# Top-10 indices of 8192 rows: result rows gathered by one-hot matmuls into one store a batch, and the last tile handled by itself

## The chip, the core and the metric

The kernel runs on one core of one Trainium2 chip. The metric is the device time of one execution in microseconds, median of several. A profiled execution also gives the span: first instruction to last. It is about 2 us below the timed figure (721.4 against 723.2 for the same run). A second figure beside each span is the mean clock granted to TensorE (PE).

## The reference

```python
x = np.random.randn(8192, 8192).astype(np.float32); k = 10
indices = np.argpartition(x, -k, axis=1)[:, -k:]
values = np.take_along_axis(x, indices, axis=1)
sorted_idx = np.argsort(-values, axis=1)
return np.take_along_axis(indices, sorted_idx, axis=1)     # int64, (8192, 10)
```

All 268 MB of x have to be read once; the result is 0.66 MB.

## The kernel before

64 tiles of 128 rows pass through a pipeline. A tile lies in SBUF, the on-chip memory of 128 partitions, with each row cut into 16 pieces of 512 columns: partition `(a q)` holds piece q of 16 rows, one after the other, and eight such sets `a` make the 128 rows. `load` brings 4 MB in four DMAs of 1 MB; `weigh` takes exponentials on ScalarE (ACT) and sums them over the 16 pieces of a row with matmuls; `choose` finds the 12 best of 512 columns on VectorE (DVE); `gather` (GpSimd, POOL) fetches the values at these columns; `spread` and `extract` (DVE, PE) line up a row's 192 candidates; `rank`, three tiles later, finds the ten best; once in eight tiles `decode` makes indices of the positions and `store` sends them.

```python
P = 128; N = 8192; R = 16; A = 8; S = 16; W = 512; KMAX = 10; G = 12; TB = 8; LAG = 3
# pools are laid out in SBUF in this order; input tiles come last
consts = tile_pool(name="consts", bufs=1)
epool  = tile_pool(name="e", bufs=3)
small  = tile_pool(name="small", bufs=2)
bpool  = tile_pool(name="batch", bufs=2)
xpool  = tile_pool(name="x", bufs=4)
# ...
def load(t):
    xts[t] = xpool.tile([P, N], fp32, tag="xt", name="xt")
    src = x[t*P:(t+1)*P, :].rearrange("(s a) (q j) -> (a q) s j", a=A, q=R)
    dst = xts[t].rearrange("p (s j) -> p s j", j=W)
    n = S // 4
    for s in range(0, S, n):
        nc.sync.dma_start(out=dst[:, s:s+n, :], in_=src[:, s:s+n, :])
# ...
def decode(b):
    # ... slot, low, hot, pick
    o = opacks[b % 2]                                   # [P, TB, KMAX, 2] u32
    nc.vector.scalar_tensor_tensor(out=o[:, :, :, 0], in0=low, scalar=float(W), in1=pick,
                                   op0=ALU.mult, op1=ALU.add)
    ready[b] = o

def store(b):
    o = ready.pop(b).rearrange("p t k two -> p t (k two)")
    for a in range(A):                                  # 8 DMAs of 10 KB, in runs of 80 bytes
        nc.scalar.dma_start(out=out_atn[a, :, b*TB:(b+1)*TB, :], in_=o[a*S:(a+1)*S, :, :])

for t in range(ntiles + LAG):
    # choose(t) interleaved with rank(t - 3); gather(t); weigh(t + 1)
    # store(any decoded batch); spread, extract(t - 1); decode if t - 3 closes a batch; load(t + 3)
```

After the loop a check of the sums decides whether a slow fallback has to run.

## Time and profile before

| | before |
|---|---|
| timed, median of the 3 runs (range) | 724.35 us (723.89 to 725.72) |
| span, clock | 721.4 us, 0.755 |
| last input byte lands (L) | 684.8 us |
| from L to the end (the tail) | 36.6 us |
| rate of the load stream | 408 GB/s |
| bytes missing in dips of that rate | 20.2 us worth |
| time of a load packet (2 KB) | 84 ns, from the 1st to the 99th percentile |

L is read from the trace's DMA records, the dips from the bytes below 408 GB/s in bins of 1 us. The prediction's L, 685.2, is the completion of the last load, 0.3 us after its last packet. The engines run in parallel, so with a DMA row of nines and a flat GB/s row, read the loads first: their bytes over their rate is the least the stream can take, and everything else counts only where it interrupts the stream or follows it.

Two views of the kernel before that the prediction does not show. From the page, the load queue (packets, MB, share of the 16 DMA engines) and the DMA issues (count, KB each, median us from issue to landing):

```profile
q1 hardware_dynamic: 135168, 268.45, 97.5%
...
xt<-in_x_dram SPq DMA_DIRECT2D x256, 1024.0 KB, 13.5
out_dram<-opack ACTq DMA_DIRECT2D x64, 10.0 KB, 5.4
```

And the issue of the loads in the view of the input tile (duration in ns: least, median, most; first and last start):

```profile
L83 SPq DMA_DIRECT2D xt<-in_x_dram x256: 367/2442/5356, 0.7 to 671.6; - x128
```

The median issue takes 2.44 us, and 1 MB at 408 GB/s takes 2.57: the issuer is held to about the pace of the stream, so this median is a number to compare between kernels.

### The profile page before, as it was taken

The numbers are of one execution on the slowest core, as the hardware profiler recorded it, in microseconds if no ns is written. First come the engines' busy times: TensorE is split into PE (matmuls) and PEld (weight loads), VectorE is DVE, ScalarE is ACT, GpSimd is POOL, SyncE is SP. The second block draws the span as 40 slices with busy tenths as digits, with TensorE's granted clock in tenths as the row PEclk, the third lists the DMA queues.
The fourth block names the chain that finished last, engine by engine and source line by source line (L and its number), as shares of the span: only waits on it lengthen the run. The fifth ranks groups of instructions, "written<-read, shape, count | busy, mean of one in ns | idle before, by whom it ended". The sixth has DMA issues, their size and how long they took to land.

```text
span 721.4 us, 7720 instructions
## 1 busy us (share of the span) xinstructions
PE 541.0 (75%) x2562; PEld 323.0 (45%) x2562; DVE 456.9 (63%) x1288; ACT 488.2 (68%) x258; POOL 65.6 (9%) x71
## 2 busy tenths in 40 slices
PE   2577888877787787777888677777787968776963
PEld 0243554444354454344555344434454634443652
DVE  1545666856677566774677576576567657676574
ACT  4776777667777667667777577767767667776720
POOL 0010111010011011011011101101101101110110
PEclk9885666677788588875758678888758677888675
DMA  9999999999999999999999999999999999999900
GB/s 336 409 407 409 407 408 407 406 333 408 407 409 346 395 407 408 408 353 409 407 409 407 345 406 409 407 405 358 408 408 407 348 402 408 408 409 338 382 1 6
DMA packets 144569, 269.62 MB, mean 374 GB/s; under 512 B 13456, under 2 KB 13456, under 8 KB 144528
## 3 DMA queue, kind: packets, MB, share of 16 engines
q1 hardware_dynamic: 135168, 268.45, 97.5%
q10 hardware_dynamic: 9360, 0.67, 0.9%
q8 instruction: 20, 0.33, 0.2%
q14 instruction: 21, 0.17, 0.1%
HBM read 268.45 MB, written 0.66 MB: 373 GB/s over the span
## 4 chain that ended last, share of the span: by engine, by line
SPq 77%; DMA 16%; issue 3%; DVE 1%; PE 1%; ACT 1%; POOL 0%; DVEq 0%; ACTq 0%
SPq L83 77%; DMA xt<-in_x_dram 16%; PE g L183 1%; ACT e L124 1%; PE s L132 0%; DVE masked L174 0%; DVE hot L214 0%; POOL cand L161 0%; DVE g L194 0%; DVE wall L147 0%; DVE posb L196 0%; DVE cidb L150 0%; DVE m L148 0%; DVE t8a L193 0%; DVE hot L218 0%
## 5 line engine op out<-in xcount | busy, mean ns | idle before, releaser
L124 ACT ACTIVATE e<-xt,bias 128x4096 bf16<-128x4096 f32 x128 | 474.7, 3709 | 192.3 <-DMA xt<-in_x_dram 169.4
L132 PE MATMUL s<-e,group 128*128 128x512 bf16 x1024 | 359.8, 517 | 163.4 <-ACT e L124 163.4
L132 PEld LDWEIGHTS <-group 128*128 128x128 bf16 x1024 | 129.6, 129 | 367.4 <-issue 322.6
L183 PEld LDWEIGHTS g<-cpack,masked 128*128 128x128 f32 x1536 | 203.8, 211 | 18.9 <-issue 10.7
L147 DVE MAX8 wall<-s 128x8 f32<-128x512 f32 x64 | 44.8, 699 | 248.5 <-PE s L132 248.4
L183 PE MATMUL g<-cpack,masked 128*128 128x16 f32 x1536 | 195.8, 273 | 5.2 <-DVE masked L174 5.2
L161 POOL INDIRECT_COPY cand<-xt,idx 128x192 f32 x64 | 64.9, 1014 | 635.9 <-issue 438.7
L174 DVE TENSOR_TENSOR masked<-cand,cpack 128x1536 f32<-128x1536 f32 x64 | 111.9, 1748 | 2.6 <-POOL cand L161 2.6
L150 DVE FIND_INDEX8 cidb<-wall,s 128x8 uint16<-128x512 f32 x64 | 44.1, 689 | 0.0
L152 DVE FIND_INDEX8 cidb<-wall,m 128x8 uint16<-128x512 f32 x64 | 43.8, 684 | 0.0
L148 DVE MATCH_REPLACE8 m<-wall,s 128x512 f32<-128x512 f32 x64 | 43.5, 680 | 0.0
L151 DVE MAX8 wall<-m 128x8 f32<-128x512 f32 x64 | 43.1, 674 | 0.0
L193 DVE MAX8 t8a<-g 128x8 f32<-128x192 f32 x64 | 22.2, 348 | 3.6 <-PE g L183 3.6
L124 ACT ACTIVATION_READ_ACCUMULATOR e<-xt,bias 128x1 f32 x128 | 23.8, 186 | 0.0
L196 DVE FIND_INDEX8 posb<-t8a,g 128x8 uint16<-128x192 f32 x64 | 22.8, 355 | 0.0
L198 DVE FIND_INDEX8 posb<-t8b,g 128x8 uint16<-128x192 f32 x64 | 22.5, 351 | 0.0
L194 DVE MATCH_REPLACE8 g<-t8a,g 128x192 f32<-128x192 f32 x64 | 22.2, 347 | 0.0
L197 DVE MAX8 t8b<-g 128x8 f32<-128x192 f32 x64 | 21.9, 342 | 0.0
L264 ACT ACTIVATE e<-tall,bias 128x64 f32<-128x64 f32 x1 | 0.3, 348 | 22.2 <-DVE tall L199 22.2
L153 DVE TENSOR_SCALAR idx<-cidb,cpack 128x12 uint16<-128x12 uint16 x64 | 13.6, 213 | 0.1
L222 DVE TENSOR_REDUCE pick<-hot 128x80 f32<-128x960 f16 x8 | 9.2, 1152 | 0.2
L199 DVE COPY tall<-t8b 128x1 f32<-128x1 f32 x64 | 9.3, 145 | 0.0
(29 smaller groups left out, 54.3 us busy)
## 6 DMA issues: line engine op xcount, KB each, us to landing
xt<-in_x_dram SPq DMA_DIRECT2D x256, 1024.0 KB, 13.5
out_dram<-opack ACTq DMA_DIRECT2D x64, 10.0 KB, 5.4
cpack<-topk_cpack ACTq DMA_DIRECT2D x1, 12.5 KB, 2.4
```

Source lines behind the costliest of these rows:

```text
L83: nc.sync.dma_start(out=dst[:, s:s + n, :], in_=src[:, s:s + n, :])
L124: nc.scalar.activation(out=e.rearrange("p s j -> p (s j)"), in_=xt[:, h * SP_ * W:(h + 1) * SP_ * W], func=ACTF.Exp, bias=bias[:, 0:1], sc ...
L132: nc.tensor.matmul(ss[t], lhsT=group[:, s, :], rhs=e[:, i, :], start=s == 0, stop=s == S - 1)
L147: lambda: nc.vector.max(out=w16[:, 0:8], in_=m),
L148: lambda: nc.vector.match_replace(out=m2, in_to_replace=w16[:, 0:8], in_values=m, imm_value=-1.0),
L150: lambda: nc.vector.max_index(out=cid[:, 0:8], in_max=w16[:, 0:8], in_values=m),
L151: lambda: nc.vector.max(out=w16[:, 8:16], in_=m2),
L152: lambda: nc.vector.max_index(out=cid[:, 8:16], in_max=w16[:, 8:16], in_values=m2),
L161: nc.gpsimd.add_instruction(mybir.InstIndirectCopy(name=nc.get_next_instruction_name(), ins=[nc.gpsimd.lower_ap(xts[t]), nc.gpsimd.lower_a ...
L174: nc.vector.tensor_tensor(out=masked[t], in0=cands.pop(t).unsqueeze(2).to_broadcast(shape), in1=own.unsqueeze(1).unsqueeze(3).to_broadcast ...
L183: nc.tensor.matmul(gs[t][:, c, :], lhsT=mk[:, c, :, :].rearrange("p a s -> p (a s)"), rhs=place, start=True, stop=True)
L196: lambda: nc.vector.max_index(out=pos[:, 0:8], in_max=t8a, in_values=g),
```

## The change

The intent has three parts. The store leaves as one DMA whose runs are 640 bytes; its rows are brought together by a mask and eight one-hot matmuls. The last tile is a batch by itself, so that seven tiles are decoded before it. The last tile is weighed in five parts, and loaded in eight pieces (the first tile too), so that less work follows the last byte.

```diff
-    out_atn = out_u32.rearrange("(t s a) n -> a s t n", s=S, a=A)
+    out_rows = out_u32.rearrange("(r a) n -> r (a n)", a=A)
+    starts = list(range(0, ntiles, TB)) + [last]
     ...
-        n = S // 4
+        n = S // (8 if t in (0, last) else 4)
     ...
-    cpack = consts.tile([P, A + R + 1], fp32)
+    cpack = consts.tile([P, P + R + 1], fp32)
     ...
+    send = consts.tile([P, TB, TB * S], fp32)
+    nc.vector.memset(send, 0.0)
+    for i in range(TB):
+        nc.vector.tensor_copy(out=send[:, i, i * S:(i + 1) * S], in_=place)
     ...
+        parts = [S // 4, S // 4, S // 4, S // 8, S // 8] if t == last else [S // 2, S // 2]
     ...
+        picked[b] = bpool.tile([P, TB, A, KMAX], fp32, tag="rows", name="rows")
+        nc.vector.tensor_tensor(
+            out=picked[b][:, 0:n], in0=val.unsqueeze(2).to_broadcast(shape),
+            in1=own_a.unsqueeze(1).unsqueeze(3).to_broadcast(shape), op=ALU.mult,
+        )
+    def deliver(b):
+        ...
+        for i in range(n):
+            nc.tensor.matmul(fo, lhsT=send[:, i, 0:n * S],
+                             rhs=rows[:, i].rearrange("p a k -> p (a k)"),
+                             start=i == 0, stop=i == n - 1)
     def store(b):
-        for a in range(A):
-            nc.scalar.dma_start(
-                out=out_atn[a, :, b * TB:(b + 1) * TB, :], in_=o[a * S:(a + 1) * S, :, :]
-            )
+        nc.vector.tensor_copy(out=o[:, :, :, 0],
+                              in_=ready.pop(b).rearrange("p (a k) -> p a k", k=KMAX))
+        nc.scalar.dma_start(out=out_rows[r0:r0 + n * S, :],
+                            in_=o.rearrange("p a k two -> p (a k two)"))
     ...
+        run(rank_steps(last - 2))
+        run(rank_steps(last - 1))
+        decode(batch_of[last - 1])
+        deliver(batch_of[last - 1])
+        store(batch_of[last - 1])
+        spread(last)
+        extract(last)
+        run(rank_steps(last))
+        decode(batch_of[last])
+        deliver(batch_of[last])
+        store(batch_of[last])
```

More of the change, by code (lines that the diff above doesn't have):

```diff
@@ L16 @@
 W = N // R
+BANK = 512
 KMAX = 10
 G = 12
-PIECES = 2
-SP_ = S // PIECES
 TB = 8
@@ L73 @@
     )
-    xts, ss, gs, idxs, cands, masked, batch, ready = {}, {}, {}, {}, {}, {}, {}, {}
+    last = ntiles - 1
+    starts = list(range(0, ntiles, TB)) + [last]
+    sizes = [b - a for a, b in zip(starts, starts[1:] + [ntiles])]
+    batch_of = {t: b for b, t0 in enumerate(starts) for t in range(t0, t0 + sizes[b])}
+    xts, ss, gs, idxs, cands, masked, batch = {}, {}, {}, {}, {}, {}, {}
+    picked, ready = {}, {}
     def load(t):
@@ L88 @@
     part = np.arange(P)
-    own_np = (part[:, None] // R == np.arange(A)[None, :]).astype(np.float32)
+    own_np = (part[:, None] // R == part[None, :] // S).astype(np.float32)
     place_np = (part[:, None] % R == np.arange(R)[None, :]).astype(np.float32)
@@ L93 @@
     cpack_dram = nc.inline_tensor(np.ascontiguousarray(cpack_np), name="topk_cpack")
-    cpack = consts.tile([P, A + R + 1], fp32)
+    cpack = consts.tile([P, P + R + 1], fp32)
     nc.scalar.dma_start(out=cpack, in_=cpack_dram.ap())
-    own, place, base = cpack[:, 0:A], cpack[:, A:A + R], cpack[:, A + R:A + R + 1]
+    own, place, base = cpack[:, 0:P], cpack[:, P:P + R], cpack[:, P + R:P + R + 1]
+    own_a = own.rearrange("p (a s) -> p a s", s=S)[:, :, 0]
     bias = consts.tile([P, 1], fp32)
@@ L105 @@
         nc.vector.tensor_copy(
-            out=group[:, s, :].rearrange("p (a s) -> p a s", s=S)[:, :, s], in_=own
+            out=group[:, s, :].rearrange("p (a s) -> p a s", s=S)[:, :, s], in_=own_a
         )
+    send = consts.tile([P, TB, TB * S], fp32)
+    nc.vector.memset(send, 0.0)
+    for i in range(TB):
+        nc.vector.tensor_copy(out=send[:, i, i * S:(i + 1) * S], in_=place)
     slots_i = consts.tile([P, G], i32)
@@ L113 @@
     tall = consts.tile([P, ntiles], fp32)
-    eall = consts.tile([P, ntiles, PIECES], fp32)
-    opacks = [consts.tile([P, TB, KMAX, 2], u32, name=f"opack{i}") for i in range(2)]
+    nsums = 2 * ntiles + 3
+    eall = consts.tile([P, nsums], fp32)
+    opacks = [consts.tile([TB * S, A, KMAX, 2], u32, name=f"opack{i}") for i in range(2)]
     for o in opacks:
@@ L119, in weigh @@
     def weigh(t):
-        xt = xts[t]
         ss[t] = spsum.tile([P, W], fp32, tag="s", name="s")
-        for h in range(PIECES):
-            e = epool.tile([P, SP_, W], bf16, tag="e", name="e")
+        parts = [S // 4, S // 4, S // 4, S // 8, S // 8] if t == last else [S // 2, S // 2]
+        s0 = 0
+        for h, n in enumerate(parts):
+            e = epool.tile([P, S // 2, W], bf16, tag="e", name="e")
             nc.scalar.activation(
-                out=e.rearrange("p s j -> p (s j)"),
-                in_=xt[:, h * SP_ * W:(h + 1) * SP_ * W],
+                out=e[:, 0:n, :].rearrange("p s j -> p (s j)"),
+                in_=xts[t][:, s0 * W:(s0 + n) * W],
                 func=ACTF.Exp, bias=bias[:, 0:1], scale=BETA,
-                accum_out=eall[:, t, h:h + 1],
+                accum_out=eall[:, 2 * t + h:2 * t + h + 1],
             )
-            for i in range(SP_):
-                s = h * SP_ + i
-                nc.tensor.matmul(ss[t], lhsT=group[:, s, :], rhs=e[:, i, :],
-                                 start=s == 0, stop=s == S - 1)
+            for i in range(n):
+                for j in range(0, W, BANK):
+                    nc.tensor.matmul(ss[t][:, j:j + BANK], lhsT=group[:, s0 + i, :],
+                                     rhs=e[:, i, j:j + BANK],
+                                     start=s0 + i == 0, stop=s0 + i == S - 1)
+            s0 += n
     def choose_steps(t):
         m = ss.pop(t)
-        if t % TB == 0:
-            batch[t // TB] = (
+        b = batch_of[t]
+        i = t - starts[b]
+        if i == 0:
+            batch[b] = (
                 bpool.tile([P, TB, 16], u16, tag="cidb", name="cidb"),
@@ L141, in choose_steps @@
             )
-        cid = batch[t // TB][0][:, t % TB, :]
+        cid = batch[b][0][:, i, :]
         w16 = wall[:, t, :]
@@ L159, in gather @@
     def gather(t):
-        cands[t] = small.tile([P, G, S], fp32, tag="cand", name="cand")
+        cands[t] = small.tile([P, G, 16], fp32, tag="cand", name="cand")
         nc.gpsimd.add_instruction(
@@ L165, in gather @@
                 outs=[nc.gpsimd.lower_ap(cands[t].rearrange("p g s -> p (g s)"))],
-                num_valid_indices=S * G,
+                num_valid_indices=16 * G,
             )
@@ L171, in spread @@
     def spread(t):
-        shape = [P, G, A, S]
+        shape = [P, G, P // 16, 16]
         masked[t] = small.tile(shape, fp32, tag="masked", name="masked")
@@ L175, in spread @@
             out=masked[t], in0=cands.pop(t).unsqueeze(2).to_broadcast(shape),
-            in1=own.unsqueeze(1).unsqueeze(3).to_broadcast(shape), op=ALU.mult,
+            in1=own.rearrange("p (c s) -> p c s", s=16).unsqueeze(1).to_broadcast(shape),
+            op=ALU.mult,
         )
@@ L187, in rank_steps @@
         g = gs.pop(t).rearrange("p c q -> p (c q)")
-        pos = batch[t // TB][1][:, t % TB, :]
+        b = batch_of[t]
+        pos = batch[b][1][:, t - starts[b], :]
         t8a = small.tile([P, 8], fp32, tag="t8a", name="t8a")
@@ L204, in decode @@
         cidb, posb = batch.pop(b)
-        slot = bpool.tile([P, TB, KMAX], u16, tag="slot")
-        low = bpool.tile([P, TB, KMAX], u16, tag="low")
-        nc.vector.tensor_scalar(out=slot, in0=posb[:, :, 0:KMAX], scalar1=R.bit_length() - 1,
+        n = sizes[b]
+        slot = bpool.tile([P, TB, KMAX], u16, tag="slot", name="slot")[:, 0:n, :]
+        low = bpool.tile([P, TB, KMAX], u16, tag="low", name="low")[:, 0:n, :]
+        nc.vector.tensor_scalar(out=slot, in0=posb[:, 0:n, 0:KMAX],
+                                scalar1=R.bit_length() - 1,
                                 scalar2=None, op0=ALU.logical_shift_right)
-        nc.vector.tensor_scalar(out=low, in0=posb[:, :, 0:KMAX], scalar1=R - 1,
+        nc.vector.tensor_scalar(out=low, in0=posb[:, 0:n, 0:KMAX], scalar1=R - 1,
                                 scalar2=None, op0=ALU.bitwise_and)
-        shape = [P, TB, KMAX, G]
-        hot = bpool.tile(shape, fp16, tag="hot")
-        pick = bpool.tile([P, TB, KMAX], fp32, tag="pick")
+        shape = [P, n, KMAX, G]
+        hot = bpool.tile([P, TB, KMAX, G], fp16, tag="hot", name="hot")[:, 0:n]
+        pick = bpool.tile([P, TB, KMAX], fp32, tag="pick", name="pick")[:, 0:n, :]
         nc.vector.tensor_tensor(
@@ L218, in decode @@
         nc.vector.tensor_tensor(
-            out=hot, in0=hot, in1=cidb[:, :, 0:G].unsqueeze(2).to_broadcast(shape),
+            out=hot, in0=hot, in1=cidb[:, 0:n, 0:G].unsqueeze(2).to_broadcast(shape),
             op=ALU.mult,
@@ L222, in decode @@
         nc.vector.reduce_sum(out=pick, in_=hot, axis=X_AX)
-        o = opacks[b % 2]
+        val = bpool.tile([P, TB, KMAX], fp32, tag="val", name="val")[:, 0:n, :]
         nc.vector.scalar_tensor_tensor(
-            out=o[:, :, :, 0], in0=low, scalar=float(W), in1=pick, op0=ALU.mult, op1=ALU.add,
+            out=val, in0=low, scalar=float(W), in1=pick, op0=ALU.mult, op1=ALU.add,
         )
-        ready[b] = o
-    def store(b):
-        o = ready.pop(b).rearrange("p t k two -> p t (k two)")
-        for a in range(A):
-            nc.scalar.dma_start(
-                out=out_atn[a, :, b * TB:(b + 1) * TB, :], in_=o[a * S:(a + 1) * S, :, :]
-            )
+        shape = [P, n, A, KMAX]
@@ new lines, in decode @@
+        picked[b] = bpool.tile([P, TB, A, KMAX], fp32, tag="rows", name="rows")
[4 more added lines that the diff above has]
+    def deliver(b):
+        n = sizes[b]
+        rows = picked.pop(b)
+        fo = fpsum.tile([P, A * KMAX], fp32, tag="fo", name="fo")[0:n * S, :]
+        for i in range(n):
+            nc.tensor.matmul(fo, lhsT=send[:, i, 0:n * S],
+                             rhs=rows[:, i].rearrange("p a k -> p (a k)"),
+                             start=i == 0, stop=i == n - 1)
+        ready[b] = fo
@@ new lines, in store, with interleave @@
+    def store(b):
+        n = sizes[b]
+        o = opacks[b % 2][0:n * S]
+        nc.vector.tensor_copy(out=o[:, :, :, 0],
+                              in_=ready.pop(b).rearrange("p (a k) -> p a k", k=KMAX))
+        r0 = starts[b] * S
+        nc.scalar.dma_start(out=out_rows[r0:r0 + n * S, :],
+                            in_=o.rearrange("p a k two -> p (a k two)"))
+    def interleave(*lists):
+        for group_ in zip(*[l for l in lists if l]):
+            for step in group_:
+                step()
@@ L236, with run @@
+    def run(steps):
+        for step in steps:
+            step()
     with tc.manual_schedule():
         weigh(0)
-        for t in range(ntiles + LAG):
-            first = choose_steps(t) if t < ntiles else []
+        for t in range(ntiles):
             second = rank_steps(t - LAG) if t >= LAG else []
-            for i in range(6):
-                for steps in (first, second):
-                    if steps:
-                        steps[i]()
-            if t < ntiles:
-                gather(t)
-                if t + 1 < ntiles:
-                    weigh(t + 1)
+            if t == last:
+                run(second)
+                second = []
+            interleave(choose_steps(t), second)
+            gather(t)
+            if t + 1 < ntiles:
+                weigh(t + 1)
@@ L249 @@
             for b in list(ready):
                 store(b)
-            if 1 <= t <= ntiles:
+            if t >= 1:
                 spread(t - 1)
                 extract(t - 1)
-            if t >= LAG and (t - LAG) % TB == TB - 1:
-                decode((t - LAG) // TB)
+            for b in list(picked):
+                deliver(b)
+            if t >= LAG and batch_of[t - LAG] != batch_of[t - LAG + 1]:
+                decode(batch_of[t - LAG])
             if t + 3 < ntiles:
                 load(t + 3)
-        for b in list(ready):
-            store(b)
+        run(rank_steps(last - 2))
@@ L263 @@
+        run(rank_steps(last - 1))
[8 more added lines that the diff above has]
+        store(batch_of[last])
     e10 = small.tile([P, ntiles], fp32, tag="e10")
     nc.scalar.activation(out=e10, in_=tall, func=ACTF.Exp, bias=bias[:, 0:1], scale=BETA)
-    good = small.tile([P, 1 + PIECES, ntiles], fp32, tag="good")
+    good = small.tile([P, nsums + ntiles], fp32, tag="good")
@@ L266 @@
     nc.vector.tensor_scalar(
-        out=good[:, 0:PIECES, :].rearrange("p a t -> p (a t)"),
-        in0=eall.rearrange("p t a -> p (t a)"), scalar1=FINITE, scalar2=None, op0=ALU.is_lt,
+        out=good[:, 0:nsums], in0=eall, scalar1=FINITE, scalar2=None, op0=ALU.is_lt,
     )
     nc.vector.scalar_tensor_tensor(
-        out=good[:, PIECES, :], in0=e10, scalar=SLACK, in1=wall[:, :, G],
+        out=good[:, nsums:nsums + ntiles], in0=e10, scalar=SLACK, in1=wall[:, :, G],
         op0=ALU.mult, op1=ALU.is_gt,
@@ L274 @@
     ngood1 = small.tile([P, 1], fp32, tag="ngood1")
-    nc.vector.reduce_sum(out=ngood1, in_=good.rearrange("p a t -> p (a t)"), axis=X_AX)
-    gps = fpsum.tile([1, 1], fp32)
+    nc.vector.reduce_sum(out=ngood1, in_=good, axis=X_AX)
+    gps = fpsum.tile([P, A * KMAX], fp32, tag="fo", name="gps")[0:1, 0:1]
     nc.tensor.matmul(gps, lhsT=ngood1, rhs=ones, start=True, stop=True)
@@ L279 @@
     nc.vector.tensor_copy(out=ngood, in_=gps)
-    checks = P * (1 + PIECES) * ntiles
+    checks = P * (nsums + ntiles)
     passed = nc.values_load(ngood[0:1, 0:1], min_val=0, max_val=checks)
```

## The prediction

> **What bounds the kernel now.** I read the page first, then the waits of the DMA queue's engine, then the stretch around one store in slices of 1 us, then the last 36 us instruction by instruction. From the page: the span, the use of the DMA engines in 40 slices of 18.0 us, and the chain that ended last.
>
> ```profile
> span 721.4 us, 7720 instructions
> ...
> DMA  9999999999999999999999999999999999999900
> GB/s 336 409 407 409 407 408 407 406 333 408 407 409 346 395 407 408 408 353 409 407 409 407 345 406 409 407 405 358 408 408 407 348 402 408 408 409 338 382 1 6
> ...
> SPq 77%; DMA 16%; issue 3%; DVE 1%; PE 1%; ACT 1%; POOL 0%; DVEq 0%; ACTq 0%
> ```
>
> The chain is the load queue: issue of loads 77%, their flight 16%. No compute engine is on it for more than 1%. Between slice 2 and slice 38 the rate is a flat 405 to 409 GB/s, with seven dips; then two slices without loads. So there are three parts: a stream that runs at its rate (268.45 MB / 408 GB/s = 658 us), seven holes in it, and a tail that no load covers. The eight stores come one per eight tiles, about 85 us apart, and seven of them fall where the seven dips are. The waits of the load queue name them:
>
> ```profile
> SPq L83 <- DMA out_dram<-opack: 64.2, 7, 9.6
> ```
>
> Seven times the queue that issues loads waited for a store to land, 9.2 us each. The rate around the first store, in slices of 1 us (columns: slice, length, busy time of each engine, granted PE clock, DMA share, GB/s):
>
> ```profile
> 143.00:144.00 1.00, 1.00 (x4) 0.41 (x3) 0.00 (x0) 0.00 (x0) 0.00 (x0) 0.50 1.10 388
> 144.00:145.00 1.00, 1.00 (x4) 0.33 (x3) 0.00 (x0) 0.09 (x1) 0.00 (x0) 0.50 1.04 290
> 145.00:146.00 1.00, 1.00 (x6) 0.53 (x4) 0.00 (x0) 1.00 (x1) 0.19 (x1) 0.70 0.62 120
> 146.00:147.00 1.00, 1.00 (x11) 1.00 (x11) 0.98 (x4) 1.00 (x1) 0.83 (x1) 1.00 0.96 78
> 147.00:148.00 1.00, 1.00 (x12) 1.00 (x11) 1.00 (x5) 1.00 (x1) 0.00 (x0) 1.00 0.70 172
> 149.00:150.00 1.00, 1.00 (x4) 0.38 (x3) 1.00 (x4) 0.00 (x0) 0.00 (x0) 0.51 1.00 285
> ```
>
> The engines run dry and then take four more microseconds to come back. Why: the built program gives its DMAs eight completion semaphores in turn. The eight 10 KB stores of a batch stand among the loads in that order, so the fourth piece of one tile's load must wait for a store, and the next tile's first piece for a load only two before it. In the trace that fourth piece went out at 144.58, when the store issued at 139.31 had landed, and the next at 147.16; the piece before had gone out at 132.87. A load needs 13.5 us from issue to landing, so a pause of 11.7 us empties the queue.
>
> The tail, in order of time (start, length, engine, line, operation):
>
> ```profile
> 685.31 3.71 ACT L124 ACTIVATE e<-xt,bias 128x4096 bf16<-128x4096 f32 x1 [1.35 <-DMA xt<-in_x_dram]
> ...
> 691.08 0.70 DVE L147 MAX8 wall<-s 128x8 f32<-128x512 f32 x1 [1.39 <-PE s L132]
> ...
> 702.15 1.76 DVE L174 TENSOR_TENSOR masked<-cand,cpack 128x1536 f32<-128x1536 f32 x1 [2.56 <-POOL cand L161]
> ...
> 704.05 5.28 PE L183 MATMUL g<-cpack,masked 128*128 128x16 f32 x24 [0.91 <-DVE masked L174]
> ...
> 709.37 0.37 DVE L193 MAX8 t8a<-g 128x8 f32<-128x192 f32 x1 [3.61 <-PE g L183]
> ...
> 715.04 3.91 ACTq L232 DMA_DIRECT2D out_dram<-opack  x8
> ```
>
> The last load lands at 685.2 (call it L) and the span ends 36.2 us later: weigh, choose (ends L+10.9), gather (L+16.9), spread, extract, rank (L+26.1), decode of eight tiles, eight store issues, landing.
>
> **What the Trainium skill says.** "DMA: Bandwidth & Descriptors", section "Issuing engines are not separate DMA queues": DMAs from all engines run on the same 16 DMA engines and interleave. The trace agrees: the first store, issued at 138.91 behind full queues, landed at 143.7 (4.8 us), while the fastest of the unhindered last ones took 1.5. Same page, "Rules for kernel authors": many small transfers should be joined into one, and under 64 KB one pays mostly overhead. Here a store is 10 KB in pieces of 80 B; yet their packets hold only 0.9% of the engines' time (6.5 us), so the trace puts the cost in the waits rather than in the bytes. "TensorE: Matmul & The Clock Gate", "What's actually happening": an idle TensorE falls to half rate and returns after some 3.4 us of sustained work. The trace agrees: the 24 extract records took 2.75 us at 690.88 with clock 1.00, and 5.27 and 5.28 us in the tail with clock 0.50, which five microseconds of extract did not lift.
>
> **The change part by part.**
> *Stores.* 64 of 10 KB in 80 B pieces become 7 of 80 KB in 640 B pieces, one of 70 and one of 10 KB. In the new built order one store takes one of the eight semaphores between two pieces of a load; the next load on that semaphore stands seven loads later, at about 2.5 us each some 17 us, and the store is issued well before it. Only 5.3 loads are in flight (13.5/2.5), so a reuse distance of seven holds nothing up. All seven dips should go. Adding up the missing bytes below 408 GB/s in 1 us bins, the dips cost 3.4, 3.2, 2.4, 2.7, 2.3, 2.9 and 3.1 us: 19.9 us. The stores' bytes stay (0.2 us a batch, already outside that sum). I allow 0.8 us for remaining disturbance and the larger constant (74 KB for 12.8 KB, 0.15 us). Stream: 19.1 us saved; L moves from 685.2 to 666.
> *Added work in the stream.* Per batch, DVE gets one multiply of 640 elements (the 1536-element one takes 1748 ns, so 0.73 us) and a copy (0.2 us); PE gets 8 f32 matmuls, 16 records at 0.12 to 0.22 us: 2 to 3.5 us in 82 us. The DVE is 63% busy. The gather that frees a buffer ended 1.0 to 5 us before the load queue wanted it in the undisturbed tiles, with about 10 us of queued loads behind that. So this is hidden.
> *Weighing in five parts.* After L one 1024-column activation (about 1.1 us with its readout) and two matmuls instead of 3.7 + 1.9. But the scores of tile 63 are then ready at about L+4, while DVE is still choosing tile 62 (ended L+2.6 before), spreading (1.7) and, newly ahead, ranking tile 60 (1.8): free at about L+5.8, as before (691.08 is L+5.9). The gain here is nearly nil. Choosing alone, not interleaved, takes 3.5 instead of 4.9: it ends at L+9.3, 1.6 earlier.
> *The tail's order.* DVE runs in program order, and before spreading tile 63 it now must: spread 62 (L+11.0), wait for a cold extract 62 (5.4: L+16.5), rank 62 (1.95: L+18.5), decode seven tiles (before 3.55 for eight; seven plus the multiply 3.9: L+22.4), wait for 7 matmuls on a cold PE (14 x 0.19 + 0.3 = 3.0: L+25.4), copy (L+25.7). Spread 63 could have begun at L+15.4, when its gather is done. Then spread (L+27.4), cold extract (L+32.8), rank (L+34.8), decode of one tile, seven small operations plus the three of the final check (1.5: L+36.3), one matmul and copy (L+37.0), one store to landing and end (2.5: L+39.5). Before it was L+36.2: 3.3 us lost. What the single store saves (3.5 us of issue) and the short decode (2.3) is more than eaten.
> *Sum.* -19.1 + 3.3 = -15.8 us: 721.4 to 705.6 in the profile, 724.35 to 708.5 us timed, a ratio of 0.978.
>
> **Rivals.**
> (a) The store's wait is not removed but moved: the ACT queue stands before the DVE copy, or a load still draws the store's semaphore. For it: ACT issues in order. Against: the copy stands right after choosing and ranking, which end about 2 us before ACT finishes the tile it is at, and the reuse distance is seven. If half of each dip stayed: 718.
> (b) The dips come from writes among the reads, not from the semaphores. For it: 285 to 307 GB/s for four microseconds after the refill, when the queue is full again. Against: at 139 to 142, stores already issued, the rate was still 406 to 412. If true, 80 KB a batch would still cost 1 to 1.5 us: 715.
> (c) The tail is not longer, because PE stays warm through it (two extracts at 2.75 and faster delivery matmuls, 6 us less) : 702. Against: over 4 us of idle PE before extract 62, the same gap that turned it cold before.
> (d) Without the pauses PE becomes the bound (75% busy, half clock about a third of the time). Against: between dips the margin of the gather does not shrink from tile to tile.
>
> **Range and chances.** The dips are measured and well explained, +-1.5 us; the tail is a hand-laid schedule, +-2.5. So 704 to 713 should hold it 8 times in 10. The 2% line is 709.9, only 1.4 us above my figure; rivals a and b lie on its slow side, c on its fast side. Faster 0.66, same 0.32, slower 0.02.
>
> **What would show it.** GB/s row flat at 405 or more from slice 2 to the last loading slice; the wait of loads for stores gone; last load at 665 to 667; the tail from there 38 to 41 us, with DVE's spread of the last tile some 10 us after its gather ended, both late extracts at 5.3 us and clock 0.5. Wrong if dips remain at the seven stores, if loads wait for the gather, or if the tail is under 36 us.

## The result and the profile after

The changed kernel is correct and slower: 750.05 us (748.03 to 750.39, 4 runs) against 724.98 us (4 runs), a ratio of 1.0341 with a 95% interval of 1.0317 to 1.0366. Ratios here are the mean time of one kernel's fast runs over that of the other's of the same rounds, so they differ a little from the ratio of the medians. The prediction was 708.5 with a range of 704 to 713.

The page after, in the order of the lines read before:

```profile
span 748.1 us, 7968 instructions
...
DMA  9999999999999999999999999999999999999400
GB/s 334 387 387 386 386 387 386 387 387 387 386 386 387 388 387 386 387 386 388 387 386 387 388 386 387 382 387 389 387 383 386 387 386 382 386 387 381 177 1 5
...
q1 hardware_dynamic: 135296, 268.45, 97.5%
...
SPq 78%; PE 7%; DMA 7%; DVE 4%; issue 2%; ACT 1%; ACTq 0%
...
xt<-in_x_dram SPq DMA_DIRECT2D x248, 1024.0 KB, 14.5
...
out_dram<-opack ACTq DMA_DIRECT2D x7, 80.0 KB, 5.4
```

The seven dips are gone from the GB/s row, as predicted. But the plateau between them went from 408 to 387, in every slice from the second on. The bytes are the same 268.45 MB, the DMA row is all nines, and the loads fill the same 97.5% of a longer span: the engines were just as busy and moved less. In the waits of the load queue (total us, times, longest) the stores have vanished and nothing has taken their place; the 49.4 us is the final check, after the last load. Under it, the issue of loads:

```profile
SPq L339 <- DVE ngood L337: 49.4, 1, 49.4
SPq L89 <- DMA xt<-in_x_dram: 1.3, 2, 0.9
```

```profile
L89 SPq DMA_DIRECT2D xt<-in_x_dram x264: 384/2582/5598, 0.8 to 695.7; - x132
```

The median issue took 2582 ns where it took 2442: 5.7% more, and no wait. In the trace's records the packets say the same. Of 131,072 load packets of 2 KB, all from the 1st to the 99th percentile took 84 ns before; after, they spread from 84 to 98 with a median of 88. So each transfer became slower, in the same queue, with the same packet sizes. 268.45 MB take 658.0 us at 408 GB/s and 693.7 at 387: 35.7 us, nearly twice what the dips had cost.

The tail, in order of time (start, length, engine, line, operation; in brackets the idle time before it and what ended it):

```profile
708.77 1.15 ACT L139 ACTIVATE e<-xt,bias 128x1024 bf16<-128x1024 f32 x1 [2.90 <-issue]
...
711.75 0.27 DVE L325 TENSOR_SCALAR good<-eall 128x131 f32<-128x131 f32 x1 [2.75 <-ACT e L139]
...
722.21 1.01 POOL L180 INDIRECT_COPY cand<-xt,idx 128x192 f32 x1 [9.11 <-issue]
...
730.27 2.90 PE L263 MATMUL fo<-rows,send 128*112 128x80 f32 x14 [6.01 <-DVE rows L252]
...
733.37 1.75 DVE L193 TENSOR_TENSOR masked<-cand,cpack 128x1536 f32<-128x1536 f32 x1
...
735.26 5.27 PE L203 MATMUL g<-cpack,masked 128*128 128x16 f32 x24 [2.09 <-DVE masked L193]
```

L is 705.8 here, the tail 42.3 us (36.6 before). The gather of the last tile ended at 723.2, and its spread began ten microseconds later, at 733.37 (L+27.5; before L+17.3): rank of tile 62, decode of seven tiles and their delivery stand ahead of it on DVE. That part was predicted. Not predicted is the head: the fourth of the five parts left ACT idle for 2.90 us although all data were there at 705.8, and DVE stood 2.75 us at `good<-eall`, an operation of the final check that the build had placed among those of rank 60 and that needs all five sums.

One more line of evidence, the stretch around L in slices of 1 us (busy time of each engine, clock, DMA share, GB/s):

```profile
699.00:700.00 1.00, 0.34 (x2) 0.19 (x2) 0.00 (x0) 1.00 (x3) 0.00 (x0) 1.00 0.89 330
...
701.00:702.00 1.00, 1.00 (x5) 0.64 (x3) 0.00 (x0) 1.00 (x3) 0.70 (x1) 0.50 0.08 29
...
704.00:705.00 1.00, 1.00 (x6) 1.00 (x6) 1.00 (x6) 1.00 (x1) 0.00 (x0) 0.50 0.07 27
```

For nearly five microseconds before L only about one sixteenth of the DMA engines works (share 0.06 to 0.08): one of the 16 is late and the tile waits for it.

### The profile page after: what moved, and what is told of

It reads as the page before. It is cut to its first block, busy times and chain, and to the rows that moved or that the text cites. A ratio compares the mean times of both kernels' runs of the same rounds, so it can differ in the third digit from the quotient of the medians.

```text
span 748.1 us, 7968 instructions
## 1 busy us (share of the span) xinstructions
PE 588.4 (79%) x2690; PEld 376.7 (50%) x2690; DVE 468.2 (63%) x1321; ACT 489.2 (65%) x264; POOL 69.5 (9%) x71
## 3 DMA queue, kind: packets, MB, share of 16 engines
q1 hardware_dynamic: 135296, 268.45, 97.5%
## 4 chain that ended last, share of the span: by engine, by line
SPq 78%; PE 7%; DMA 7%; DVE 4%; issue 2%; ACT 1%; ACTq 0%
SPq L89 78%; DMA xt<-in_x_dram 6%; PE g L203 3%; PE s L147 2%; PE fo L263 1%; ACT e L139 1%; DVE masked L193 1%; DMA out_dram<-opack 1%; DVE cidb L171 0%; DVE m L167 0%; DVE cidb L169 0%; DVE wall L166 0%; DVE g L215 0%; DVE wall L170 0%; DVE posb L217 0%
## 5 line engine op out<-in xcount | busy, mean ns | idle before, releaser
L139 ACT ACTIVATE e<-xt,bias 128x4096 bf16<-128x4096 f32 (+2 forms) x131 | 475.6, 3630 | 213.7 <-DMA xt<-in_x_dram 204.1
L147 PE MATMUL s<-e,group 128*128 128x512 bf16 x1024 | 354.2, 512 | 139.6 <-ACT e L139 139.5
L203 PEld LDWEIGHTS g<-cpack,masked 128*128 128x128 f32 x1536 | 234.7, 238 | 23.6 <-issue 15.0
L203 PE MATMUL g<-cpack,masked 128*128 128x16 f32 x1536 | 226.1, 295 | 7.2 <-DVE masked L193 7.2
L180 POOL INDIRECT_COPY cand<-xt,idx 128x192 f32 x64 | 68.8, 1075 | 653.1 <-issue 419.6
L263 PE MATMUL fo<-rows,send 128*128 128x80 f32 (+2 forms) x128 | 26.9, 397 | 9.9 <-DVE rows L252 9.9
L263 PEld LDWEIGHTS fo<-rows,send 128*128 128x128 f32 (+2 forms) x128 | 25.2, 302 | 10.1 <-DVE rows L252 6.1
L271 DVE CAST opack<-fo 128x80 uint32<-128x80 f32 (+2 forms) x9 | 2.2, 240 | 18.7 <-PE fo L263 18.7
```

Source lines behind the costliest of these rows:

```text
L139: nc.scalar.activation(out=e[:, 0:n, :].rearrange("p s j -> p (s j)"), in_=xts[t][:, s0 * W:(s0 + n) * W], func=ACTF.Exp, bias=bias[:, 0:1 ...
L147: nc.tensor.matmul(ss[t][:, j:j + BANK], lhsT=group[:, s0 + i, :], rhs=e[:, i, j:j + BANK], start=s0 + i == 0, stop=s0 + i == S - 1)
L180: nc.gpsimd.add_instruction(mybir.InstIndirectCopy(name=nc.get_next_instruction_name(), ins=[nc.gpsimd.lower_ap(xts[t]), nc.gpsimd.lower_a ...
L203: nc.tensor.matmul(gs[t][:, c, :], lhsT=mk[:, c, :, :].rearrange("p a s -> p (a s)"), rhs=place, start=True, stop=True)
L263: nc.tensor.matmul(fo, lhsT=send[:, i, 0:n * S], rhs=rows[:, i].rearrange("p a k -> p (a k)"), start=i == 0, stop=i == n - 1)
```

## The experiments

Why did the loads slow down? The added work can't hold up a load (no wait shows it), and the queue, the source addresses and the packet sizes are the same. What differs is where the tiles lie. Input tiles come after all other pools in SBUF, and the change makes the constants and batch buffers ahead of them larger. In the built programs the four tiles start at 79872 and on (multiples of 2048 bytes) before, and at 90304 and on after, 192 bytes past a multiple of 256.

The Trainium skill has a rule that bears on it: "DMA: Bandwidth & Descriptors", section "How a descriptor splits into AXI transactions", says that a descriptor is cut into transactions of 256 bytes and that one which does not start on a multiple of 256 begins with a transaction from the boundary below. By that, a 2 KB packet would take nine in place of eight (an estimate from the section). The section speaks of fetching and gives no rate.

The theories were: *place* (the address of the tiles sets the rate), against *traffic* (something in the added work, constants or stores slows the loads). For the dips, *shared semaphores* against *small writes*. For the tail, *order on DVE* against *the five parts*. Unless told otherwise a run is correct, and the ratio is to the kernel before in the same rounds.

| run | timed us (median) | ratio, 95% interval | span | clock | L | tail | load rate |
|---|---|---|---|---|---|---|---|
| after | 750.05 | 1.0341, 1.0317 to 1.0366 | 748.1 | 0.718 | 705.8 | 42.3 | 387 |
| after, tiles moved 64 B | 712.58 | 0.9841, 0.9792 to 0.9889 | 710.6 | 0.759 | 669.8 | 40.8 | 408 |
| before, tiles moved 192 B | 759.57 | 1.0480, 1.0427 to 1.0533 | 757.5 | 0.718 | 719.5 | 37.9 | 387 |
| before, moved 64 B | 759.29 (one run) | none | 757.5 | 0.715 | 720.7 | 36.8 | 387 |
| before, moved 128 B | 759.56 (one run) | none | 757.8 | 0.722 | 720.3 | 37.5 | 387 |
| eight stores a batch | 732.13 | 1.0077, 1.0018 to 1.0136 | 730.0 | 0.736 | 689.9 | 40.1 | 408 |
| two halves | 714.80 | 0.9841, 0.9802 to 0.9881 | 713.2 | 0.743 | 670.2 | 42.9 | 408 |
| last tile in its batch | 707.92 | 0.9755, 0.9716 to 0.9793 | 705.7 | 0.751 | 670.2 | 35.6 | 408 |
| last tile first | 705.15 | 0.9705, 0.9663 to 0.9747 | 703.4 | 0.770 | 670.0 | 33.4 | 408 |
| last tile first, two e buffers | 701.60 | 0.9677, 0.9651 to 0.9704 | 699.8 | 0.767 | 669.8 | 30.0 | 408 |
| in its batch, two e buffers | 709.02 | 0.9771, 0.9747 to 0.9796 | 707.4 | 0.764 | 669.8 | 37.6 | 408 |

Rows 2 to 5 shared one chip, the next four another, the last two a third. One run of the kernel before on the second chip took 1464.97 us and counts as slow; the ratios leave it out.

### The changed kernel with its tiles moved by 64 bytes

```diff
+    gap = ctx.enter_context(tc.tile_pool(name="gap", bufs=1))
+    gap.tile([P, 16], fp32, name="gap")
     xpool = ctx.enter_context(tc.tile_pool(name="x", bufs=4))
```

An unused tile of 64 bytes a partition puts the input tiles at 90368 and on: a multiple of 256, and not of 512. No instruction is added to the stream.

> The changed kernel with 64 unused bytes per partition ahead of the input tiles, so that these start at a multiple of 256 bytes again (256 past a multiple of 2048; the kernel before has multiples of 2048, the changed kernel 192 past one). Theory (place of the input tiles in the SBUF sets the rate of the loads): 2 KB packets back at 84 ns all alike, 405 to 409 GB/s, last load some 35 us earlier than in the changed kernel, span 708 to 716. Rival (place of the input in HBM, moved by the larger constant; or the pieces of 512 KB; or one slow DMA engine by chance): rate stays at 387 and the span at 746 to 750.

Its page and the issue of its loads:

```profile
span 710.6 us, 7923 instructions
...
GB/s 344 409 408 407 407 408 407 408 407 408 407 407 409 406 409 407 409 407 407 409 407 408 406 409 408 406 407 406 408 401 408 406 404 404 407 409 399 181 1 5
```

```profile
L91 SPq DMA_DIRECT2D xt<-in_x_dram x264: 437/2443/5272, 0.8 to 659.9; - x132
```

(The count of instructions is smaller because some matmul records are missing from this trace.) The rate is 408 again, the issue 2443 ns, and the packets are back at 84 ns. 64 bytes of nothing took 37.5 us off the span. The traffic theory falls: all of the change's stores, matmuls and constants are still there. Without the dips and at the full rate L is 669.8, 15.0 us earlier than before, and the tail takes 4.2 of those back. Timed, this is 1.6% under the kernel before, with an interval that reaches across the 2% line.

### The kernel before with its tiles moved by 192, 64 and 128 bytes

The same edit to the kernel before, with 48, 16 and 32 elements in the gap. It tells whether the place alone is enough, and whether the remainder matters.

> The kernel before with 192 unused bytes ahead of its input tiles, nothing else: they start 192 past a multiple of 256, as in the changed kernel. Theory (place in the SBUF): rate falls to about 387 GB/s, packets spread over 84 to 98 ns, and with the seven dips still there the span is 745 to 760. Rival (anything else of the change): nothing happens, 408 GB/s, span 720 to 724.

> As the last, with 64 bytes: tiles 64 past a multiple of 256. If any start off a multiple of 256 costs the same: about 387 GB/s. If the cost goes with the distance from 256 or only some residues cost: another rate between 387 and 408.

> As the last, with 128 bytes: tiles 128 past a multiple of 256. If any start off a multiple of 256 costs the same: about 387 GB/s; if 128 is enough: 408 GB/s and a span of 721.

The page of the first, and the wait of its load queue:

```profile
GB/s 331 387 386 387 386 387 387 386 338 387 386 387 337 373 387 386 387 307 387 386 387 386 326 386 387 386 387 339 387 386 387 342 385 387 386 387 353 361 1 6
```

```profile
SPq L85 <- DMA out_dram<-opack: 69.0, 7, 10.5
```

Plateaus at 387 and dips between them: both faults at once, 36.1 us more span than before. All three remainders cost the same (757.5, 757.5 and 757.8 us). So of the remainders tried, 0 (mod 256) gives the full rate and 64, 128 and 192 the lower one; how far off does not show. What goes on inside a transfer to such an address no run shows. The last two are single runs, but 36 us with the rate of every slice at 386 to 387 is not the noise of a single run.

### Eight stores a batch again, from the gathered rows

```diff
-        nc.scalar.dma_start(out=out_rows[r0:r0 + n * S, :],
-                            in_=o.rearrange("p a k two -> p (a k two)"))
+        for j in range(n):
+            nc.scalar.dma_start(out=out_rows[r0 + j * S:r0 + (j + 1) * S, :],
+                                in_=o[j * S:(j + 1) * S].rearrange("p a k two -> p (a k two)"))
```

On top of the moved tiles. Each store is again eight DMAs of 10 KB, but in runs of 640 bytes: the number of DMAs is that of before, the pieces are those of after.

> As the first experiment, with each gathered store sent as eight DMAs of 16 partitions (10 KB each, still in runs of 640 bytes) instead of one. Theory (the dips are waits of loads for the semaphores that the eight stores take): the built order again puts a load piece behind the second store, so seven dips of 2 to 3.5 us return, the wait of loads for stores is 50 to 70 us in the profile, span 725 to 731. Rival (the dips come from the 80 byte pieces): no dips, span 710 to 713.

Its page and its wait:

```profile
GB/s 337 409 407 408 407 408 407 408 308 408 408 408 409 325 409 407 409 406 362 408 408 408 344 404 407 408 408 298 408 408 408 407 316 408 407 409 374 286 1 5
```

```profile
SPq L91 <- DMA out_dram<-opack: 73.4, 7, 11.4
```

All seven dips come back (25.2 us worth of missing bytes, 2.1 to 5.0 each, some more than expected) and with them the wait of the loads for stores, seven times, 73.4 us where 50 to 70 were expected. The bytes and pieces are those of the kernel with one store, so writes among reads are not what costs. The number of DMAs is: eight in a row go round the eight completion semaphores that the loads use too. At the first dip the next load drew the semaphore of the second store and went out at 157.14, when that store had landed (157.12).

### The last tile weighed in two halves, loaded in four pieces

```diff
-        parts = [S // 4, S // 4, S // 4, S // 8, S // 8] if t == last else [S // 2, S // 2]
+        parts = [S // 2, S // 2]
-        n = S // (8 if t in (0, last) else 4)
+        n = S // 4
```

On top of the moved tiles (with the gap made larger, so that they stay at 90368).

> As the first experiment, with the last tile weighed in two halves and the first and last tile loaded in four pieces, as in the kernel before. Prediction on record (the five parts gain nearly nothing since DVE is not free earlier): span 710 to 713. Rival (the five parts are worth their 3.8 us): 714 or more. It also tells whether the one late DMA engine at the end comes from the smaller pieces: the last load would land at 666 instead of 669.8.

Span 713.2 against 710.6, of which the tail has 2.1 us; the timed ratio is 0.9841 for both. That is 0.2 us above the expected span and below the rival's 714. So the five parts are worth about 2 us in the profile and nothing that the timing resolves; and of these 2 us PE's clock may have up to 1.7, since the last eight matmuls of the weighing took 3.56 us in this run, where they took 1.89 in the kernel before. L is 670.2: the smaller pieces are not what makes it late.

### The last tile back in its batch of eight

```diff
-    starts = list(range(0, ntiles, TB)) + [last]
+    starts = list(range(0, ntiles, TB))
         run(rank_steps(last - 2))
+        spread(last)
+        extract(last)
         run(rank_steps(last - 1))
-        decode(batch_of[last - 1])
-        deliver(batch_of[last - 1])
-        store(batch_of[last - 1])
-        spread(last)
-        extract(last)
         run(rank_steps(last))
```

> The changed kernel with its input tiles at a multiple of 256 bytes (the first experiment, 710.6 us in the profile), and the last tile decoded and stored with its batch of eight again, in the order of the kernel before; gathered stores and five-part weighing stay. Theory (deciding the last tile by itself puts the decode of the seven others and their delivery ahead of the spread of the last one on DVE, and so lengthens the tail): the last tile's spread starts at once after its gather, 16 to 18 us after the last load instead of 26; the tail is 36.5 to 38 us instead of 40.8; span 706 to 708. Rival (the separate last tile pays): span 712 or more.

The spread of the last tile:

```profile
684.94 1.76 DVE L195 TENSOR_TENSOR masked<-cand,cpack 128x1536 f32<-128x1536 f32 x1 [2.56 <-POOL cand L182]
```

The spread now waits for its own gather (2.56 us) and not for DVE, starts at L+14.8 in place of L+26.0, and the tail, 35.6 us, is 5.2 us shorter than with the last tile decoded by itself in the change's order (spread, tail and span all came out a little better than expected). That order, and not the new store, is what lengthened the tail.

### The last tile's spread and extract ahead of the decode of the seven

```diff
         run(rank_steps(last - 2))
+        spread(last)
+        extract(last)
         run(rank_steps(last - 1))
         decode(batch_of[last - 1])
         deliver(batch_of[last - 1])
-        store(batch_of[last - 1])
-        spread(last)
-        extract(last)
         run(rank_steps(last))
         decode(batch_of[last])
         deliver(batch_of[last])
+        store(batch_of[last - 1])
         store(batch_of[last])
```

With two PSUM buffers for the delivered rows, so that the second delivery needn't wait for the first store. The decode of the seven now runs while PE extracts the last tile.

> As the first experiment, with the last tile still by itself, but its spread and extract placed ahead of the ranking of the tile before and of the decode of the seven, and a second PSUM buffer for the delivery so that the two deliveries need not wait for one another. Theory (the tail is the order of DVE's work): decode of the seven fits into the 5.3 us of the cold extract; tail 30 to 32 us, span 700 to 702, timed about 702 to 704, 3% under the kernel before. Rival (PE or the gather bounds the tail whatever the order): tail stays above 38.

The extract of tile 61, which PE does before it weighs tile 62; the fourth part of the weighing, the first of choosing, the spread, the extract, the first operation of the decode, and the rank:

```profile
667.39 5.14 PE L205 MATMUL g<-cpack,masked 128*128 128x16 f32 x24
...
674.32 1.15 ACT L141 ACTIVATE e<-xt,bias 128x1024 bf16<-128x1024 f32 x1 [4.36 <-issue]
...
678.94 0.69 DVE L168 MAX8 wall<-s 128x8 f32<-128x512 f32 x1
...
688.83 1.76 DVE L195 TENSOR_TENSOR masked<-cand,cpack 128x1536 f32<-128x1536 f32 x1 [2.56 <-POOL cand L182]
...
690.73 5.27 PE L205 MATMUL g<-cpack,masked 128*128 128x16 f32 x24 [0.90 <-DVE masked L195]
...
692.42 0.19 DVE L231 TENSOR_SCALAR slot<-posb 128x70 uint16<-128x70 uint16 x1
...
696.33 0.36 DVE L216 MAX8 t8a<-g 128x8 f32<-128x192 f32 x1
```

The decode from 692.42 to 696.3 fits into the cold extract (to 696.0), so it costs 0.3 us. The tail is 33.4 us, 7.4 below the change's order, and a little above the 30 to 32 expected. The second line tells why: the fourth part, after 4.36 us of idling ACT, came so late that choosing began at L+8.9 (L+4.9 in the run above). "issue" only says that the profile names no releaser. There are three exponential buffers and each part takes one, so parts four and five need buffers whose matmuls PE had not done. That was a guess until the next run.

### Two exponential buffers for the five parts

```diff
         for h, n in enumerate(parts):
-            e = epool.tile([P, S // 2, W], bf16, tag="e", name="e")
+            if s0 % (S // 2) == 0 or s0 % (S // 2) + n > S // 2:
+                whole = epool.tile([P, S // 2, W], bf16, tag="e", name="e")
+            at = s0 % (S // 2)
+            e = whole[:, at:at + n, :]
```

The parts (4 + 4 and 4 + 2 + 2 of 16 groups) fill two buffers. The same instructions, the same order, no buffer more.

> The last-tile-first order with one edit: the five weighing parts of the last tile fill two exponential buffers (4+4 groups and 4+2+2 groups) in place of five, so none of them has to wait until the matmuls of tile 62 have given a third buffer back. Theory (buffer wait is what cost the last-tile-first order its last microseconds): the fourth part's idle time before it, 4.36 us, goes to under 1 us; the check operation on the sums no longer holds DVE for 2.7 us; choosing of the last tile ends at L+5 to L+6 in place of L+8.9; the tail goes from 33.4 to 30 to 31.5 us, span 700 to 702, timed 1.5 to 3.5 us under the last-tile-first order (ratio to before about 0.966 to 0.968). Rival (the extracts of the waiting tiles on a cold TensorE, in program order ahead of the last tile's, set the end): choosing comes earlier but the spread of tile 63 and its extract start no earlier than now, and the tail stays at 33 us.

> The order with the last tile decoded in its batch of eight, with the same edit (two exponential buffers for the five parts). There choosing already ended at L+4.9, so the buffer theory expects at most 1 us: tail 34.5 to 35.6, span 704.5 to 706, ratio to before 0.973 to 0.976. If it gains as much as the other one does, the wait for a buffer was in its tail too and was not what delayed choosing in the other alone. The difference between these two runs, 4 to 5 us expected, is then the worth of a separate decode of the last tile once its order is right.

With the last tile first, the extract of tile 61, the fourth part, the check's operation, the first of choosing, and the spread:

```profile
666.69 3.27 PE L208 MATMUL g<-cpack,masked 128*128 128x16 f32 x24
...
669.65 1.13 ACT L144 ACTIVATE e<-xt,bias 128x1024 bf16<-128x1024 f32 x1
...
673.78 0.20 DVE L330 TENSOR_SCALAR good<-eall 128x131 f32<-128x131 f32 x1
...
675.35 0.69 DVE L171 MAX8 wall<-s 128x8 f32<-128x512 f32 x1
...
685.24 1.76 DVE L198 TENSOR_TENSOR masked<-cand,cpack 128x1536 f32<-128x1536 f32 x1 [2.56 <-POOL cand L185]
```

No part waits, the check's operation holds nobody up, choosing begins at L+5.5 and the spread at L+15.4. The tail is 30.0 us and the time 701.60: the fastest kernel, 3.2% under the kernel before. That the wait was for buffers is shown: its 4.36 us are gone, here and in the other run below, where PE was as slow as in the run above. How much of the 3.4 us off the tail they bought is not. The two runs differ in a second thing: the extract of tile 61 took 5.14 us above and 3.27 here. With 5.14 us in both (the run above and the other one with two buffers, whose orders agree up to this point), choosing began at L+8.9 and L+6.9, so 2.0 us are the buffers' and the rest may be PE's clock. The rival, that the spread would come no earlier, falls: it began at L+18.8 above. The timed ratios, 0.9705 and 0.9677, have intervals that overlap. (The text on record said that choosing ends at L+5 to L+6 "in place of L+8.9". Both are times at which it begins; the slip is in the word.)

The same edit to the order in one batch missed its expectation: tail 37.6, where 34.5 to 35.6 was expected, though its timed ratio (0.9771) can't be told from that without the edit (0.9755). There the extract of tile 61 came upon a cold PE, 5.14 us where it had been 2.75, and choosing began at L+6.9. So the tail moves by about 2 us with the state of PE's clock at the moment the stream ends, which no edit here controls. (In the changed kernel PE had matmuls without a pause from 701.8 to 712.5, and its clock was 0.50 until 711.2.) Between the two orders with two buffers lie 7.6 us in the profile, where 4 to 5 were expected, and 0.94% in the timed ratios (about 6.8 us; the intervals are apart): a separate decode of the last tile pays, once its spread does not wait for the others.

## Why the prediction was wrong, and where it was right

From the predicted span of 705.6 us the measured one is reached in three steps. The changed kernel with moved tiles separates them:

| step | us |
|---|---|
| predicted span | 705.6 |
| last load at 669.8 in place of 666 | +3.8 |
| tail 40.8 in place of 39.5 | +1.3 |
| rounding | -0.1 |
| changed kernel, tiles moved by 64 bytes | 710.6 |
| tiles at 192 past a multiple of 256: last load +36.0, tail +1.5 | +37.5 |
| changed kernel | 748.1 |

(By the prediction's own L, the completion of the last load, the first two terms are 4.1 and 0.9 us.)

**The step that failed** is "Stream: 19.1 us saved; L moves from 685.2 to 666". It took the 408 GB/s between the dips as given and subtracted from there. The larger constants were weighed by their bytes ("the larger constant (74 KB for 12.8 KB, 0.15 us)") and the added buffers not at all; nobody asked what they push along. They pushed the input tiles off a multiple of 256 bytes, and the stream lost 5.1% of its rate: L came to 705.8. Why a transfer to such an address is slower stays open. None of the four rivals spoke of the rate of the undisturbed stream. Without this (the kernel with moved tiles) the time was 712.58, inside the range, at its slow end.

**The seven dips** all went, for the reason given. Rival (a), a wait that moves, is refuted by the load queue's waits; rival (b), writes among reads, by the run with eight stores of the same bytes, where the dips return. Rival (d), PE as the bound, is refuted by a flat 404 to 409 in nearly all loading slices.

**L at 666** was still 3.8 us too early. One of the 16 engines ends later and later when nothing lets it catch up: in the moved kernel, the last of a load's 16 completions came 0.7 us after the 15th at 56 us, 1.5 at 269, 2.6 at 451 and 3.8 at 661. In the kernel before it is 1.1 us at most. Its queue runs empty at each store, and that lets the late engine catch up: in the run with eight stores, the moved kernel but for the number of stores, the 16th completion came 1.4 us after the 15th at most and 0.1 at 660. So the dips paid back a part of what they cost; taking away 20.2 us of them moved L by 15.0. Why one engine is slower stays open; it is not the smaller pieces of the last tile (the run with four pieces has it too), and the records used do not tell which engine it is.

**The tail** was right in its mechanism and nearly in its size: the spread at L+26.0 in the moved kernel (predicted 25.7), a 2.9 us wait for the delivery (3.0), extracts of 5.27 us at half clock (5.3), 40.8 us in all (39.5). Rival (c), a warm PE, did not come. What the working missed is that five parts need five exponential buffers and there are three, and that an operation of the check had been placed among those of rank 60. Both cost little in the moved kernel (the fourth part waited 1.46 us there) and more in the kernel with the last tile first (4.36 us of waiting).

**Weighing in five parts**, "nearly nil", came out at about 2 us in the profile, PE's clock included, and zero in the timing. **The added work in the stream** was hidden, as said, and sized rightly: in the moved kernel a delivering matmul record took 357 ns on average, but they overlap, and the 112 of the seven large batches kept PE busy for 20.3 us, 2.9 a batch (2 to 3.5 predicted). The margin of the gather is thinner than the prediction took it to be: with the stream at its full rate the loads waited for the gather three times, 0.9 us in all, in the moved kernel, and seven times, 5.6 us in all, with the last tile in its batch.

## What to carry to other kernels

A new constant or buffer also moves whatever is laid out after it: when a kernel is bound by its loads, compare the start addresses of the load targets in the two builds before predicting anything, and pad to 256 bytes (or lay out the big tiles first, which no run here tried). In this profile a fall of the plateau of the GB/s row at an unchanged DMA share meant slower transfers, and dips in it an interrupted stream; the two needed different remedies. In a tail, lay out each engine's program order by what is ready first, and count the buffers that a finer split takes.

## What the Trainium skill lacked or had wrong

- "DMA: Bandwidth & Descriptors", section "How a descriptor splits into AXI transactions": it describes the fetching of a descriptor that does not start on a multiple of 256 bytes, without a rate. Here a *destination* in SBUF off by 64, 128 or 192 bytes takes the load stream of 2 KB packets from 408 to 387 GB/s (5.1%), packets from 84 ns to a median of 87 to 88. By an estimate from the section's rule the three offsets would cost 66, 68 and 70 beats of 32 bytes for 64, or nine transactions for eight; the measured loss is the same for all three and smaller than one in eight.
- "SBUF — State Buffer", section "Operand start alignment": it tells what is legal and says that its runs timed nothing. The speed is worth a line there: 36.1 us of 721.4 for 192 bytes.
- No page that I found: loads and stores that take completion semaphores in turn can make a load wait for a store. Eight small stores in a row cost 2.3 to 3.4 us of stream each time (64.2 us of waiting in the load queue, seven times); one store of the same bytes costs none.
- "DMA: Bandwidth & Descriptors", section "Latency and other measured facts": two usually slower engines are put down, as a best guess, to DMAs issued by GpSimd. In an uninterrupted stream issued by SyncE one engine in sixteen had fallen behind by 3.8 us after 661 us, and at the end worked alone for four to five microseconds at 25 to 29 GB/s. Which engine it is, and why, is open.
